# Strassen units of a fp32 transformer block: four of a unit's seven products in one PSUM bank, copied out by ScalarE

## The chip, the cores and the metric

The kernel runs on one core of a Trainium2 chip. The metric is the device time of one execution in microseconds (us). The times before are 2052.94, 2047.32 and 2055.45 us, with a median of 2052.94. The profile is of one execution on the chip. Engines are named as the profile names them: PE is TensorE's matmul, PEld its weight load, DVE is VectorE, ACT is ScalarE, POOL is GpSimd and SP is SyncE, which issues the DMAs.

## The reference

One decoder block over 1024 tokens of width 1024, all in fp32: a Mamba-2 (SSD) branch and a gated linear attention (GLA) branch merged by gates, cross attention to 256 memory tokens, and a SwiGLU FFN, with an RMSNorm ahead of each.

```
def hybrid_mixer(n, w_in, ...):
    proj = n @ w_in
    z, xBC, dt_raw, q, k, v, r, a1, g_ssd, g_gla = jnp.split(proj, idx, axis=-1)
    y_ssd = ssd_mixer(z, xBC, dt_raw, conv_w, conv_b, dt_bias, A_log, D_skip, ssd_norm)
    y_gla = gla_mixer(q, k, v, r, a1, gla_w_a2, gla_b_a, gla_norm)
    merged = jax.nn.sigmoid(g_ssd) * (y_ssd @ w_up_ssd) + jax.nn.sigmoid(g_gla) * (y_gla @ w_up_gla)
    return merged @ w_o

def swiglu(n, w_ffn_in, w_ffn_out):
    g, u = jnp.split(n @ w_ffn_in, 2, axis=-1)
    return (jax.nn.silu(g) * u) @ w_ffn_out

h = h + hybrid_mixer(rmsnorm(h, norm_mix), ...)
h = h + mem_cross_attention(rmsnorm(h, norm_xattn), rmsnorm(mem, norm_mem), w_xq, w_xkv, w_xo)
h = h + swiglu(rmsnorm(h, norm_ffn), w_ffn_in, w_ffn_out)
return rmsnorm(h, norm_final)
```

## The kernel before

**Precision.** An fp32 product is made of three matmuls in the faster fp32r format: both factors are split into a high and a low part, and `hi*hi`, `hi*lo` and `lo*hi` are summed in PSUM. For a weight, ScalarE copies out the high part `whi` (L217) and VectorE or POOL subtracts it from the weight to get `wlo` (most subtractions and additions of VectorE and POOL have line 73, that of a helper that counts their load). `whi` and `wlo` lie in rings of three buffers.

**Units.** The projections out of `w_in` and the FFN's gate and up projections are cut into 48 Units of 256 output columns by 1024 tokens (26 in `w_in`, 22 in the FFN). A Unit computes its 2 x 2 block product with the seven products of the Strassen-Winograd scheme instead of eight. Products are called B11, B21, B22 and T1 to T4 by their right-hand operand: Bij is a block of the input, T1 to T4 are sums and differences of such blocks, held ready, already split, as `B11h`, `B11l`, `T1h` and so on by the class Operands. The left-hand sums of weights (`sa`, or `raw` in place) are made by VectorE or POOL shortly before they are split. A product is twelve matmuls, four steps of the inner dimension times three; it is one [128, 512] tile in one PSUM bank. The four results of a Unit are the quarters q(i, j) of a buffer `o` (i is the half of the columns, j that of the tokens).

**Banks and evacuation.** There are four buffers `acc` for products (and four `bank` for all else). A Unit names three for itself, and two products that share a bank are added up in it, since only the first matmul of a bank clears it. So in bank x B21 is summed onto B11, in w B22 onto T1, and in y T3 onto T2 and T4 onto both. Behind each product the bank's sum so far is taken out: a copy by ScalarE behind B11 (L348) and B21 (L350), an addition into a quarter by VectorE behind the other five. PE may write a bank's next product only when the sum before has been taken out. A quarter that has had its last part is handed on: q(0, 0) behind B21, q(1, 1) behind T3, q(1, 0) behind T4, and q(0, 1) behind B22 or T2, whichever is later.

**Order.** `group` issues the products of one Unit in the order SPACED, or those of two Units together (the FFN's first gate and up) in the order CHAIN, product by product in turn. `singles` does Units one after the other. `run` mixes the Units' steps with a side job at a given rate: the preparation of decays and gates (`ssd_prep`, `gla_prep`) beside the four z Units, the convolution of the Unit before (`conv`) beside each of six xBC Units, the SSD scan of sixteen chunk-and-group steps beside nine Units, the GLA scan beside six. Splitting a weight and taking out a product are written with a raised priority (`ahead`). In the end a scheduler fixes the order of instructions on each engine ahead of time: each engine then works strictly through its own list, and an instruction that waits holds up those behind it.

**Lines the text speaks of.** L799, L800, L804 and L807 are the bias, abs, Exp and Ln of `gla_prep` (`gx`, `gy`), L463 the Silu of a z quarter, L728 that of a convolved channel row `cv`, L893 to L895 are the decay of an SSD step (eight Relu into `e`, Exp of `e`, Exp of `csb`, which a DMA brings). ScalarE needs another table in some changes of function, an ACT_TABLE_LOAD. L51 is every matmul, L55 every transpose.

Of the kernel before, what the change touches and what calls it, by code (L numbers as in the profile page):

```python
# [12 lines left out]
AF = mybir.ActivationFunctionType  # L13
# [24 lines left out]

CHAIN = ("B11", "B21", "T1", "B22", "T2", "T3", "T4")
SPACED = ("B11", "T1", "T2", "B21", "T3", "B22", "T4")  # L40


class Tensor:
# [35 lines left out]
def block_kernel(ctx: ExitStack, tc: tile.TileContext, t: dict, out: bass.AP):  # L79
    nc = tc.nc  # L80
    now = [0.0]
    PE, ACT, SP = Tensor(nc.tensor, now), nc.scalar, nc.sync
    DVE, POOL = Meter(nc.vector, now, 0.06, 1.04e-3), Meter(nc.gpsimd, now, 0.08, 2.25e-3)

    def either(ap, slack=0.0):

        return POOL if POOL.after(ap) - slack < DVE.after(ap) else DVE
# [34 lines left out]
    def acc():  # L122
        return ps.tile([P, 512], F32, name="acc", tag="acc", bufs=4)

    def bank(dt=F32):
        return ps.tile([P, 512], dt, name="bank", tag="bank", bufs=4)

    add = lambda e, o, a, b: e.tensor_tensor(o, a, b, ALU.add)
    sub = lambda e, o, a, b: e.tensor_tensor(o, a, b, ALU.subtract)
    mul = lambda e, o, a, b: e.tensor_tensor(o, a, b, ALU.mult)  # L130
    ahead = lambda: tc.high_priority(offset=AHEAD)
# [10 lines left out]
    def slot(key, shape=(P, 2, TOK), dt=F32, name="sl"):  # L142
        pl, n = slots[key]
        return pl.tile(list(shape), dt, name=name, tag="sl", bufs=n)
# [71 lines left out]
    def split(src, hi, lo, e=None):  # L216
        ACT.activation(hi, src, AF.Copy)  # L217
        sub(e or DVE, lo, src, hi)

    def wring():  # L220
        hi = wp.tile([P, 528], F32R, name="whi", tag="whi", bufs=3)
        lo = wp.tile([P, 528], F32R, name="wlo", tag="wlo", bufs=3)
        return hi, lo

    class Operands:
# [14 lines left out]
        def __init__(s, hb, kh, first=None, key="op", swap=0, last_key=None, order=None):  # L240
            s.B, s.kh, s.key, s.done, s.swap = {}, kh, key, 0, swap
            s.order = order or tuple(s.PLAN)
            s.last_key = last_key or key
            s.steps = s.build(hb, kh, first or (lambda *a: None))
# [7 lines left out]
        def __getitem__(s, name):  # L252
            s.upto((s.order.index(name) + 1) * s.kh)
            return s.B[name]

        def build(s, hb, kh, first):
            blk = hb if callable(hb) else lambda: hb
            for name in s.order:
                new, of, comb = s.PLAN[name]
                o = s.B[name] = [slot(s.last_key if name == "T4" else s.key, (P, kh, HALF), F32R, name=name + x) for x in "hl"]  # L260
                for k in range(kh):
# [8 lines left out]
    class Unit:  # L270
# [1 line left out]

        BANK = {"B11": "x", "B21": "x", "T1": "w", "B22": "w", "T2": "y", "T3": "y", "T4": "y"}

        def __init__(s, W, row0, c0, kh=4, post=None, key="aux", okey=None, side=None):
            s.W, s.row0, s.c0, s.kh, s.post, s.key, s.okey, s.side = W, row0, c0, kh, post, key, okey or key, side or key
# [30 lines left out]
        def q(s, i, j):  # L309
            return s.o[:, i, half(j)]  # L310
# [4 lines left out]

        def step(s, name, B, cs=ALL, again=False):
            s.load()
            kh = s.kh
            if name == "B11":
                s.banks, s.swap, s.u = {}, B.swap, False  # L320
                s.out()
            if again:
                wh, wl = s.w
            else:
                with ahead():
                    src = s.left(name)
                    hi, lo = wring()
                    s.w = wh, wl = [x[:, :kh * P].rearrange("p (k c) -> p k c", c=P) for x in (hi, lo)]
                    split(src, wh, wl)
            xh, xl = B[name]  # L330
            key = s.BANK[name]
            fresh = key not in s.banks
            if fresh:
                s.banks[key] = acc()
            p = s.banks[key]
            m = 0
            for k in range(kh):
                for x, y in ((wh, xh), (wh, xl), (wl, xh)):
                    PE.matmul(p[:, cs], x[:, k, :], y[:, k, cs], start=fresh and m == 0, stop=m == 3 * kh - 1,
                              skip_group_check=True)  # L340
                    m += 1
            s.evac(name, p, cs)

        def evac(s, name, p, cs):
            q = lambda i, j: s.q(i, j ^ s.swap)[:, cs]
            with ahead():
                if name == "B11":
                    ACT.activation(q(1, 0), p, AF.Copy)  # L348
                elif name == "B21":
                    ACT.activation(q(0, 0), p, AF.Copy)  # L350
                elif name == "T1":
                    add(DVE, q(1, 1), p, q(1, 0))
                elif name in ("B22", "T2"):
                    add(DVE, q(0, 1), p, q(0, 1) if s.u else q(1, 0))
                elif name == "T3":
                    add(DVE, q(1, 1), p, q(1, 1))
                else:
                    add(DVE, q(1, 0), p[:, cs], q(1, 0))
            s.done(name, cs)

        def done(s, name, cs=ALL):

            ij = {"B21": (0, 0), "T3": (1, 1), "T4": (1, 0)}.get(name)
            if name in ("B22", "T2"):
                ij = (0, 1) if s.u else None
                s.u = True
            if ij and cs == ALL:
                s.fin(ij[0], ij[1] ^ s.swap)

    class PartUnit(Unit):  # L370


        def __init__(s, base, *a, **kw):
            super().__init__(*a, **kw)
            s.base = base

        def evac(s, name, p, cs):
            q = lambda i, j: s.q(i, j ^ s.swap)
            b = lambda i, j: s.base.q(i, j ^ s.swap)
            get = lambda i, j: settle(s.base, i, j ^ s.swap)  # L380
            if name == "B21":
                get(0, 0)
                with ahead():
                    add(DVE, q(0, 0), p, b(0, 0))
                return s.done(name)
            super().evac(name, p, cs)
            for ij in {"T1": ((1, 1),), "B22": ((0, 1), (1, 0))}.get(name, ()):
                get(*ij)
                add(either(p), q(*ij), q(*ij), b(*ij))

    lag = [1]
    posts = {}
# [1 line left out]
    def settle(*key):  # L394

        k = key if key else next(iter(posts), None)
        if k in posts:
            del posts[k]
            u, i, j = k
            u.post(i, j, u.q(i, j))  # L400
# [9 lines left out]
    def group(units, B, then=(), nxt=None, frm=6, products=7):  # L410


        for u in units:
            u.load()
        then = list(then)
        many = len(units)
        for n, name in enumerate((CHAIN if many > 1 else SPACED)[:products]):
            for x, u in enumerate(units):
                u.step(name, B)
                if many > 1:  # L420
                    B.upto((n + 1) * B.kh - (-(x + 1) * B.kh // many))
                if n == 6 and nxt:
                    nxt.upto((x + 1) * nxt.kh // many)
                if n >= frm and then:
                    then.pop(0).load()
                while len(posts) > lag[0]:
                    settle()
                    if n < 4:
                        break
                yield  # L430
        for u in then:
            u.load()
# [106 lines left out]
    for k in range(NB):  # L539
        p = bank()  # L540
# [82 lines left out]
    B = Operands(hb, 4, xnorm)  # L623
# [85 lines left out]
    cs = cp.tile([P, P], F32, name="cs")  # L709
# [452 lines left out]
    def dense(no, ins, post, pre=lambda o, j: None, js=JS):  # L1162

        todo = [(o, j) for o in range(NB) for j in js]
        nxt = pre(*todo[0])
        for n, (o, j) in enumerate(todo):
            w = left[NB * no + o]
            cur, nxt = nxt, pre(*todo[n + 1]) if n + 1 < len(todo) else None
            p = acc()
            m = 0  # L1170
            for k in range(NB):
                for a, b in ((0, 0), (0, 1), (1, 0)):
                    PE.matmul(p, w[:, a, k], ins[k][:, b, half(j)], start=m == 0, stop=m == 3 * NB - 1)
                    m += 1
            with ahead():
                post(o, j, p, cur)
            yield
# [67 lines left out]
    def residual(store, stats, gain, put):  # L1245
        def post(o, j, p, q):
            add(DVE, q, p, q)
            SP.dma_start(store[o * P:(o + 1) * P, half(j)], q)
            put(o, j, q, col(gain, o))
            stats.take(j, q)  # L1250
        return post
# [98 lines left out]
    for n in range(len(at) + 2):  # L1350
        a = at[n] if n < len(at) else None
        b = at[n - 1] if 0 < n <= len(at) else None
# [55 lines left out]
    b_xo = blocks(o_xo)  # L1408
# [1 line left out]
    def put_xo(o, j, q, g):  # L1410
        ACT.activation(b_xo[o][:, half(j)], q, AF.Copy, scale=g)

    B = Operands(b_xo, 4, order=("B11", "T1", "B21", "B22", "T2", "T3", "T4"))
    for n, _ in enumerate(dense(4, i_xo, residual(h2_d, u_xo_stats, "norm_ffn", put_xo), gate_of(h1_d), js=(1, 0))):
        if n >= 8:
            B.upto(n - 7)
# [144 lines left out]
    for x, (n, k, kn) in enumerate(todo):  # L1561
        name = CHAIN[n]
# [4 lines left out]
        cs = slice(0, 256) if n == 6 else ALL  # L1567
# [9 lines left out]
    cs = slice(256, 512)  # L1577
# [43 lines left out]
```

## Time and profile before

| | us | share of the span |
|---|---|---|
| median of three runs | 2052.94 | |
| span of the profiled execution | 2047.0 | |
| PE busy | 1955.7 | 96% |
| VectorE busy | 1321.9 | 65% |
| ScalarE busy | 846.6 | 41% |
| POOL busy | 709.0 | 35% |

The span is the profiled execution's own time, from its first to its last instruction. A busy PE says that matmuls were under way, so the gaps on PE are the time in which something else set the pace; a row of a timeline gives the start, the duration, the engine, the line, the operation with its output and inputs, and in brackets the idle time ahead of it and what ended that. The stages, in order of time: memory keys and values and the input's norm (to 128), values (to 193), z Units (193 to 296), xBC Units with the convolution (296 to 424), SSD with Units (to 683), GLA with Units (to 869), dense products and attention (to 1377), the FFN's gate and up (to 1800), its down projection (to the end).

### The profile page before, as it was taken

The page shows a single profiled execution, that of the slowest core. Times are in us where ns is not written, and L with a number is a line of the kernel's source. Part 1 is how long each engine was busy: PE and PEld are TensorE (multiplying, and loading weights), DVE is VectorE, ACT ScalarE, POOL GpSimd, SP SyncE. Part 2 cuts the span into 40 slices and gives each one's busy share as a digit, 9 for nine tenths or more (in the row PEclk, how much of TensorE's full clock was granted, in tenths as well). Part 3 has the DMA queues.
Part 4 walks back from the last instruction along what each step waited for, and adds up shares of the span by engine and source line. Part 5 has one row for each costly group of instructions (what it writes and reads, how often), then busy time and mean ns, then how long its engine had stood idle before and what let it go on. Part 6 is the DMA issues. An engine that isn't in the chain of part 4 may idle for free.

```text
span 2047.0 us, 26356 instructions
## 1 busy us (share of the span) xinstructions
PE 1955.7 (96%) x9740; PEld 1624.7 (79%) x9740; DVE 1321.9 (65%) x1876; ACT 846.6 (41%) x1477; POOL 709.0 (35%) x513
## 2 busy tenths in 40 slices
PE   7589999999999999999999999999999999999998
PEld 7589777777777777878878888887888888887887
DVE  4975569878886665542454326568777777784465
ACT  6333753355553445442223225444333333354243
POOL 0733245445554221232224300154454454430002
PEclk9799999999999999999999999999999999999999
DMA  7532242345653665496675521332323422266463
GB/s 249 181 98 76 84 144 93 113 155 174 201 166 114 195 180 166 154 324 205 219 267 198 175 93 32 118 119 83 123 77 101 131 77 93 98 236 223 154 229 131
DMA packets 246436, 309.59 MB, mean 151 GB/s; under 512 B 18058, under 2 KB 165748, under 8 KB 246308
## 3 DMA queue, kind: packets, MB, share of 16 engines
q1 hardware_dynamic: 246308, 307.92, 45.6%
q8 instruction: 76, 1.25, 0.3%
q14 instruction: 52, 0.43, 0.1%
HBM read 211.07 MB, written 96.80 MB: 150 GB/s over the span
## 4 chain that ended last, share of the span: by engine, by line
PE 71%; DVE 9%; DMA 7%; issue 4%; ACT 4%; POOL 3%; SPq 1%; POOLq 0%; DVEq 0%; ACTq 0%
PE acc L51 62%; PE bank L51 8%; DVE wlo L73 2%; PE bank L55 1%; DVE cv L73 1%; DVE o L73 1%; DMA sr<-sr_d 1%; DMA csb<-cs_d 1%; DVE hs L73 1%; DMA bd<-bd_d 1%; SPq L644 1%; ACT e L893 1%; DMA ga<-ys_d 1%; POOL raw L73 1%; DMA fr<-act_d 1%
## 5 line engine op out<-in xcount | busy, mean ns | idle before, releaser
L51 PE MATMUL acc<-hl,wd 128*128 128x512 f32 x1920 | 443.8, 393 | 9.0 <-ACT hl L217 8.4
L51 PEld LDWEIGHTS acc<-hl,wd 128*128 128x128 f32 x1920 | 362.6, 189 | 86.0 <-ACT hl L217 9.7
L73 DVE TENSOR_TENSOR wlo<-raw,whi 128x512 fp32r<-128x512 f32 x272 | 236.6, 877 | 82.8 <-ACT whi L217 78.2
L217 ACT ACTIVATE whi<-raw 128x512 fp32r<-128x512 f32 x272 | 169.8, 628 | 255.1 <-PE acc L51 214.4
L73 DVE TENSOR_TENSOR o<-acc,o 128x512 f32<-128x512 f32 (+1 forms) x256 | 173.0, 677 | 120.1 <-PE acc L51 109.1
L73 POOL TENSOR_TENSOR sa<-raw 128x512 f32<-128x512 f32 x56 | 83.2, 1486 | 223.0 <-DMA raw<-in_w_ffn_out_dram 77.8
L51 PE MATMUL acc<-fs 128*128 128x512 f32 (+1 forms) x792 | 156.0, 356 | 1.9 <-ACT o L1516 1.7
L51 PEld LDWEIGHTS acc<-fs 128*128 128x128 f32 x792 | 130.7, 189 | 22.9 <-ACT o L1516 2.1
L73 POOL TENSOR_TENSOR sa<-sa,raw 128x512 f32<-128x512 f32 x48 | 73.3, 1527 | 160.0 <-DVE wlo L73 160.0
L217 ACT ACTIVATE fs<-fr 128x1024 fp32r<-128x1024 f32 (+1 forms) x84 | 80.1, 984 | 112.8 <-PE acc L51 42.2
L73 DVE TENSOR_TENSOR fs<-fr,fs 128x1024 fp32r<-128x1024 f32 (+1 forms) x84 | 99.0, 1206 | 39.8 <-ACT fs L217 39.5
L217 ACT ACTIVATE whi<-sa 128x512 fp32r<-128x512 f32 x96 | 60.4, 630 | 133.3 <-PE acc L51 67.7
L73 POOL TENSOR_TENSOR raw<-raw,sa 128x512 f32<-128x512 f32 x48 | 63.1, 1315 | 136.4 <-DVE wlo L73 136.4
L73 POOL TENSOR_TENSOR raw<-raw 128x512 f32<-128x512 f32 x68 | 101.8, 1502 | 9.5 <-DVE sa L73 6.2
L73 DVE TENSOR_TENSOR wd<-raw,wd 128x1024 fp32r<-128x1024 f32 x40 | 51.2, 1285 | 66.7 <-ACT wd L217 66.5
L73 DVE TENSOR_TENSOR wlo<-sa,whi 128x512 fp32r<-128x512 f32 x96 | 81.0, 844 | 11.0 <-ACT whi L217 9.8
L51 PE MATMUL acc<-T3h,whi 128*128 128x512 f32 x192 | 76.9, 401 | 10.7 <-DVE o L73 10.6
L73 DVE TENSOR_TENSOR ga<-acc,ga 128x512 f32<-128x512 f32 x64 | 43.6, 686 | 67.1 <-PE acc L51 47.1
L51 PE MATMUL acc<-B21h,whi 128*128 128x512 f32 x192 | 77.5, 404 | 3.7 <-ACT o L348 3.7
L51 PE MATMUL acc<-B22h,wlo 128*128 128x512 f32 x192 | 77.0, 401 | 1.9 <-DVE wlo L73 1.9
L51 PE MATMUL acc<-T4h,whi 128*128 128x512 f32 x192 | 76.7, 399 | 2.1 <-DVE o L73 2.1
L51 PE MATMUL acc<-T2h,wlo 128*128 128x512 f32 x192 | 76.4, 398 | 1.8 <-DVE wlo L73 1.8
(372 smaller groups left out, 4809.3 us busy)
## 6 DMA issues: line engine op xcount, KB each, us to landing
raw<-in_w_in_dram SPq DMA_DIRECT2D x26, 1024.0 KB, 5.7
raw<-in_w_ffn_in_dram SPq DMA_DIRECT2D x22, 1024.0 KB, 8.5
act_d<-o SPq DMA_DIRECT2D x77, 256.0 KB, 2.0
fr<-act_d SPq DMA_DIRECT2D x35, 512.0 KB, 6.2
raw<-in_w_ffn_out_dram SPq DMA_DIRECT2D x11, 1024.0 KB, 8.7
fr<-down_d SPq DMA_DIRECT2D x20, 512.0 KB
down_d<-raw SPq DMA_DIRECT2D x33, 256.0 KB, 2.9
raw<-in_w_xkv_dram SPq DMA_DIRECT2D x8, 1024.0 KB
```

The source lines that it names most:

```text
L51: return s.e.matmul(o, x, y, **kw)
L55: return s.e.transpose(o, x, i)
L73: return f(*a, **kw)
L217: ACT.activation(hi, src, AF.Copy)
L644: SP.dma_start(r_[:, :, o:o + n], w_in[512 * h:512 * h + 512, c0:c0 + n].rearrange("(k p) c -> p k c", p=P))
L893: ACT.activation(s.e[:, h], s.csb[:, h], AF.Relu, bias=cs[:, s.i0 + h:s.i0 + h + 1], scale=-1.0)
```

## The change

All seven products keep their operands and their matmuls. Banks and evacuations are dealt anew: B11, T2, T3 and T4 share the bank c and are summed up in it, T1 and B22 share w as before, and B21 has the bank x alone. ScalarE copies the bank's sum out behind B11 into q(0, 0), T1 into q(1, 1), T2 into q(0, 1) and T4 into q(1, 0); VectorE adds behind B21 into q(0, 0), T3 into q(1, 1) and B22 into q(0, 1). Per Unit these are four copies and three additions instead of two copies and five additions. A pair of Units now takes the order PAIRED; the operands ahead of the FFN are prepared in the same order. A class that nothing uses, PartUnit, is removed.

```
 SPACED = ("B11", "T1", "T2", "B21", "T3", "B22", "T4")
+PAIRED = ("B11", "T1", "B21", "T2", "T3", "B22", "T4")
...
-        BANK = {"B11": "x", "B21": "x", "T1": "w", "B22": "w", "T2": "y", "T3": "y", "T4": "y"}
+        BANK = {"B11": "c", "T2": "c", "T3": "c", "T4": "c", "T1": "w", "B22": "w", "B21": "x"}
...
                 if name == "B11":
-                    ACT.activation(q(1, 0), p, AF.Copy)
+                    ACT.activation(q(0, 0), p, AF.Copy)
                 elif name == "B21":
-                    ACT.activation(q(0, 0), p, AF.Copy)
+                    add(DVE, q(0, 0), p, q(0, 0))
                 elif name == "T1":
-                    add(DVE, q(1, 1), p, q(1, 0))
-                elif name in ("B22", "T2"):
-                    add(DVE, q(0, 1), p, q(0, 1) if s.u else q(1, 0))
+                    ACT.activation(q(1, 1), p, AF.Copy)
+                elif name == "T2":
+                    ACT.activation(q(0, 1), p, AF.Copy)
                 elif name == "T3":
                     add(DVE, q(1, 1), p, q(1, 1))
+                elif name == "B22":
+                    add(DVE, q(0, 1), p, q(0, 1))
                 else:
-                    add(DVE, q(1, 0), p[:, cs], q(1, 0))
+                    ACT.activation(q(1, 0), p, AF.Copy)
...
-        for n, name in enumerate((CHAIN if many > 1 else SPACED)[:products]):
+        for n, name in enumerate((PAIRED if many > 1 else SPACED)[:products]):
...
-    B = Operands(b_xo, 4, order=("B11", "T1", "B21", "B22", "T2", "T3", "T4"))
+    B = Operands(b_xo, 4, order=PAIRED)
```

The instructions that a whole program issues change little: on VectorE `o<-acc,o` goes from 248 to 152, on ScalarE `o<-acc` from 100 to 196, ScalarE's table loads go from 28 to 31, and ten `o<-o` move from VectorE (75 to 65) to POOL (29 to 39). But the scheduler's lists also change. Three places follow; line numbers behind the change are one more than before for L51, L55 and L217, and L728, L799, L800, L804, L807 and L463 have become L707, L778, L779, L783, L786 and L442.

ScalarE's list over one xBC Unit, before (`sa` and `raw` are weights to be split, L348 and L350 the copies behind B11 and B21):

```order
L217 ACTIVATE whi<-raw 128x512
L217 ACTIVATE whi<-sa 128x512 x2
L217 ACTIVATE whi<-raw 128x512
L348 ACTIVATE o<-acc 128x512
L728 ACTIVATE cv<-cv 128x1024
L217 ACTIVATE whi<-raw 128x512 x3
L350 ACTIVATE o<-acc 128x512
L728 ACTIVATE cv<-cv 128x1024
```

and of the change, where L361, L349, L353 and L355 are the copies behind T4 of the Unit before, B11, T1 and T2:

```order
L218 ACTIVATE whi<-raw 128x512 x2
L218 ACTIVATE whi<-sa 128x512
L361 ACTIVATE o<-acc 128x512
L218 ACTIVATE whi<-sa 128x512
L218 ACTIVATE whi<-raw 128x512
L349 ACTIVATE o<-acc 128x512
L707 ACTIVATE cv<-cv 128x1024
L218 ACTIVATE whi<-raw 128x512
L353 ACTIVATE o<-acc 128x512
L218 ACTIVATE whi<-raw 128x512
L355 ACTIVATE o<-acc 128x512
L707 ACTIVATE cv<-cv 128x1024
```

Each copy stands behind the split of the next weight, and T2's is ahead of the second Silu.

ScalarE's list in the z Units, around the first Exp of the gates, before:

```order
L217 ACTIVATE whi<-sa 128x512
L463 ACTIVATE o<-o 128x512
L804 ACT_TABLE_LOAD
L804 ACTIVATE gy<-gy 128x2048
L217 ACTIVATE whi<-raw 128x512
L348 ACTIVATE o<-acc 128x512
L807 ACT_TABLE_LOAD
L807 ACTIVATE gy<-gy 128x2048
L217 ACTIVATE whi<-raw 128x512
L799 ACTIVATE gx<-bank,cols 128x512 x3
```

and of the change, from right behind the Exp to the copy behind B11 of the third z Unit (L349; L361 is the copy behind T4 of the second):

```order
L218 ACTIVATE whi<-sa 128x512
L778 ACTIVATE gx<-bank,cols 128x512 x3
L442 ACT_TABLE_LOAD
L442 ACTIVATE o<-o 128x512
L786 ACT_TABLE_LOAD
L786 ACTIVATE gy<-gy 128x2048
L779 ACTIVATE gy<-gx 128x1024
L361 ACTIVATE o<-acc 128x512
L779 ACTIVATE gy<-gx 128x1024
L218 ACTIVATE whi<-sa 128x512
L218 ACTIVATE whi<-raw 128x512
L349 ACTIVATE o<-acc 128x512
```

Between Exp and the copy behind B11 there stood one split; now three `gx`, two table loads, a Silu, the Ln, two abs, a copy and three splits stand there. A little further on, both loads, the second Exp and the second Ln stand ahead of the split of T3's weight and of the copy behind T2.

PE's list where the SSD stage begins (`bank<-e,xd` is the first matmul of scan step 0, and `e` its decay), before, from the end of B21's matmuls:

```order
L51 MATMUL acc<-B21l,whi 128x512
L51 MATMUL acc<-B21h,wlo 128x512
L51 MATMUL acc<-B21h,whi 128x512
L51 MATMUL bank<-e,xd 64x128 x2
L51 MATMUL bank<-xc,bt 128x512
L51 MATMUL bank<-bc 128x128
```

and of the change, from the end of T1's:

```order
L52 MATMUL acc<-T1h,whi 128x512
L52 MATMUL acc<-T1l,whi 128x512
L52 MATMUL acc<-T1h,wlo 128x512
L52 MATMUL bank<-e,xd 64x128 x2
L52 MATMUL bank<-xc,bt 128x512
L52 MATMUL bank<-bc 128x128
```

Before, all twelve matmuls of T2 and ten of B21 stood ahead of the scan step; now they come behind it.

More of the change, by code (lines that the diff above doesn't have):

```diff
@@ L319, in step @@
             if name == "B11":
-                s.banks, s.swap, s.u = {}, B.swap, False
+                s.banks, s.swap = {}, B.swap
                 s.out()
@@ L347, in evac @@
                 if name == "B11":
-                    ACT.activation(q(1, 0), p, AF.Copy)
+                    ACT.activation(q(0, 0), p, AF.Copy)
                 elif name == "B21":
-                    ACT.activation(q(0, 0), p, AF.Copy)
+                    add(DVE, q(0, 0), p, q(0, 0))
                 elif name == "T1":
-                    add(DVE, q(1, 1), p, q(1, 0))
-                elif name in ("B22", "T2"):
-                    add(DVE, q(0, 1), p, q(0, 1) if s.u else q(1, 0))
+                    ACT.activation(q(1, 1), p, AF.Copy)
+                elif name == "T2":
+                    ACT.activation(q(0, 1), p, AF.Copy)
                 elif name == "T3":
                     add(DVE, q(1, 1), p, q(1, 1))
+                elif name == "B22":
+                    add(DVE, q(0, 1), p, q(0, 1))
                 else:
-                    add(DVE, q(1, 0), p[:, cs], q(1, 0))
+                    ACT.activation(q(1, 0), p, AF.Copy)
             s.done(name, cs)
         def done(s, name, cs=ALL):
[L363 to L366, printed above, removed]
+            ij = {"B21": (0, 0), "T3": (1, 1), "B22": (0, 1), "T4": (1, 0)}.get(name)
             if ij and cs == ALL:
                 s.fin(ij[0], ij[1] ^ s.swap)
[L370 to L389, printed above, removed]
     lag = [1]
```

## The prediction

> **What bounds the kernel now.** I read the page's busy shares first, then a stretch of the span without gaps, then whom PE waits for.
>
> ```profile
> span 2047.0 us, 26356 instructions
> PE 1955.7 (96%) x9740; PEld 1624.7 (79%) x9740; DVE 1321.9 (65%) x1876; ACT 846.6 (41%) x1477; POOL 709.0 (35%) x513
> ```
>
> PE is busy for 96% and the change leaves its matmuls as they are, so all that can be won are PE's 91 us of gaps, and only those behind an evacuation of a product. The span is 2047.0 us; the runs of this kernel are 2047.32, 2052.94 and 2055.45, so the profiled execution lies 5.9 under their median. I work out a change against the profiled execution and add it to the median. The FFN shows a stretch without any gap:
>
> ```profile
> 1415.50:1800.00 384.50, 384.50 (x1663) 312.76 (x1662) 294.19 (x360) 130.90 (x221) 179.82 (x119) 1.00 0.29 97
> L73 DVE TENSOR_TENSOR o<-acc,o 128x512 f32<-128x512 f32 x248 | 169.8, 686 | 109.5 <-PE acc L51 98.5 <-issue 10.4 <-ACT o L348 0.7
> L348 ACT ACTIVATE o<-acc 128x512 f32<-128x512 f32 x48 | 27.9, 580 | 1.7 <-PE acc L51 1.7
> ```
>
> The columns behind a stretch are its length, then busy time of PE, PEld, DVE, ACT and POOL, then PE's clock. 384.50 us hold 1663 matmuls, so one takes 0.231 us and a product of twelve 2.77 us. An add behind a product takes VectorE 0.69 us, a copy takes ScalarE 0.58 us. Where PE waits for the adds is seen in the conv stage and the stage ahead of it:
>
> ```profile
> PE acc L51 <- DVE o L73: 10.6, 8, 1.5
> PE acc L51 <- DVE wlo L73: 3.7, 2, 1.9
> PE acc L51 <- ACT whi L217: 0.3, 1, 0.3
> 316.40:337.60 21.20, 19.69 (x85) 15.73 (x85) 18.76 (x19) 7.41 (x11) 10.55 (x7) 1.00 0.29 99
> ```
>
> These are 193 to 443 us: 10.6 of the 14.6 us are waits for `o`, and a conv unit keeps VectorE busy for 88% of its 21.20 us, ScalarE for 35%.
>
> **B: six conv units.** One unit on VectorE, and PE beside it:
>
> ```profile
> 328.76 3.33 DVE L73 SCALAR_TENSOR_TENSOR cv<-o,cols,cv 128x1023 f32<-128x1023 f32 x2
> 332.01 0.68 DVE L73 TENSOR_TENSOR wlo<-raw,whi 128x512 fp32r<-128x512 f32 x1
> 332.62 0.68 DVE L73 TENSOR_TENSOR o<-acc,o 128x512 f32<-128x512 f32 x1
> 333.22 2.00 DVE L73 SCALAR_TENSOR_TENSOR cv<-o,cols,cv 128x1022 f32<-128x1022 f32 x1
> 335.14 1.77 DVE L73 TENSOR_TENSOR wlo<-raw,whi 128x512 fp32r<-128x512 f32 x1
> 336.83 0.68 DVE L73 TENSOR_TENSOR o<-acc,o 128x512 f32<-128x512 f32 x1
> ...
> 332.42 0.39 PE L51 MATMUL acc<-T2h,wlo 128*128 128x512 f32 x1
> ...
> 335.66 0.39 PE L51 MATMUL acc<-B22l,whi 128*128 128x512 f32 x1
> 337.56 0.50 PE L51 MATMUL acc<-T3h,whi 128*128 128x512 f32 x1 [1.51 <-DVE o L73]
> ```
>
> T2 leaves PE at 332.8, but its add starts at 336.83, behind T1's add, a conv step and a wlo; T3 wants T2's bank at 335.89 and gets it at 337.56. That is 1.67 us, and the idle rows of the six units read 1.48 to 1.53. Now ScalarE empties the bank. Ahead of T2's copy in its row stand a Silu, two whi, and T1's copy:
>
> ```profile
> 330.93 1.06 ACT L728 ACTIVATE cv<-cv 128x1024 f32<-128x1024 f32 x1 [2.75 <-DVE cv L73]
> 334.17 0.63 ACT L217 ACTIVATE whi<-raw 128x512 fp32r<-128x512 f32 x1 [1.66 <-POOL raw L73]
> ```
>
> The Silu ends at 332.0. Even if both whi, T1's copy and T2's copy all come behind T2's end at 332.8, that is 332.8 + 2 x 0.53 (pitch of whi) + 0.5 + 0.58 = 334.9, 1.0 before T3 wants the bank. The next thing late is VectorE: it loses two adds per unit (1.2 us of pitch) and has 17.6 us of work in a unit that now takes 19.5. Carrying the rows along the new order, B21's wlo is the tightest, 0.6 us ahead of PE. So **6 x 1.67 = -10.0 us**. Bounds: -11 (also the starts behind the stalls) and 0 (a wlo that comes 0.6 + 1.67 later takes the stall's place); -10 is nearer, as ScalarE and wlo both have slack in these rows.
>
> **A: the z units beside the gate preparation.** ScalarE runs Exp and Ln of 2048 columns there.
>
> ```profile
> 231.87 1.20 PE L51 MATMUL bank<-a1T,wa 48*128 48x512 f32 x4
> 241.56 0.96 PE L51 MATMUL bank<-a1T,wa 48*128 48x512 f32 x3
> ...
> 238.30 1.28 ACT L804 ACT_TABLE_LOAD   x1
> 239.59 1.91 ACT L804 ACTIVATE gy<-gy 128x2048 f32<-128x2048 f32 x1
> 246.16 1.83 ACT L799 ACTIVATE gx<-bank,cols 128x512 f32<-128x512 f32 x3
> 248.39 2.00 ACT L800 ACTIVATE gy<-gx 128x1024 f32<-128x1024 f32 x2
> ...
> 255.27 0.50 PE L51 MATMUL acc<-B22h,wlo 128*128 128x512 f32 x1 [1.91 <-DVE wlo L73]
> 256.77:260.18 3.41, 3.41 (x10) 2.65 (x9) 3.12 (x5) 3.38 (x3) 1.56 (x3) 0.50 0.88 352
> ```
>
> A stretch of 3.41 us at half clock follows the 1.91 us gap (ten matmuls instead of 15): it costs 1.7 us. Before, the stage loses 5.5 us of idle (14.6 less the six conv stalls of about 1.51), some 1.0 in the starts of those five, and 1.7: 8.2. In the new order PE makes the first four gate products two products earlier, at 231.87 - 2 x 2.77 = 226.3, and the next three (before: at 241.56, behind T1) ahead of the unit's last product, so all the gate work reaches ScalarE sooner. From there ScalarE's new row runs gx and abs to 231.0, whi to 231.6, load and Exp to 235.2 (1.28 + 1.83), whi and three gx to 237.5, load and Silu to 239.4, load and Ln to 242.5, abs, T4's copy, abs to 245.0, then whi of T2 and of B21, and only then B11's copy, to 246.6. T2 needs that copy. PE leaves T1 at about 241.2, a little before the 241.56 of now, as those three products are done: a wait of 5.4, and 1.7 for the half clock behind. Behind it, T3's whi and T2's copy stand behind Exp and Ln with both loads (6.2 us): they end at 256.8 where PE arrives at about 254.2, so 2.6, and 1.7 again. 11.4 - 8.2 = **+3.2 us**; bounds 0 (Exp slips behind the copies as waits fall out) and +6 (a third gap like those). All that is queued behind the late copies are whi, and PE waits for these too, so nothing hides it.
>
> The Trainium skill, "TensorE: Matmul & The Clock Gate", Part 1, has the clock fall after an idle window of about 3.4 us. The trace disagrees, with a half clock right behind a gap of 1.91 us; by the page the second gap would cost no clock, A would come to +1.5 and the sum to 1.7 us less than mine.
>
> **C: entry of the SSD stage.** Before, T2 and ten matmuls of B21 stand on PE ahead of scan 0; now it stands right behind T1.
>
> ```profile
> 433.81 2.45 ACT L893 ACTIVATE e<-csb,cs 128x128 f32<-128x128 f32 x8 [2.25 <-DMA csb<-cs_d]
> 437.28 1.28 ACT L894 ACT_TABLE_LOAD   x1
> 438.57 1.06 ACT L894 ACTIVATE e<-e 128x1024 f32<-128x1024 f32 x1
> 439.54 1.05 ACT L895 ACTIVATE csb<-csb 128x1024 f32<-128x1024 f32 x1
> 439.67 1.36 DVE L73 TENSOR_TENSOR e<-e,cbm 128x1024 f32<-128x1024 f32 x1 [1.56 <-ACT e L894]
> ...
> 436.77 0.40 PE L51 MATMUL acc<-T2h,whi 128*128 128x512 f32 x1
> ...
> 441.99 0.44 PE L51 MATMUL bank<-e,xd 128*64 128x128 f32 x4
> ```
>
> PE is through T1 at 436.77, scan 0 has `e` at 441.0 (439.67 + 1.36): 4.2 us, and 1.7 for the clock: **+5.9 us**. T2 and B21 then follow without a wait, so nothing comes back. Bounds 0 (csb lands earlier by as much, since it is issued behind the conv stage's last stores) and +6 (a second gap between the scan's own matmuls is no part of it).
>
> **D: SSD stage, 443 to 683.** Sixteen decays, each 2.45 + 1.28 + 1.06 + 1.05 = 5.8 us on ScalarE, now run among four copies per unit instead of two. A bank's copy has 2.77 us of another product as its cover: a copy behind a whole decay is 3.1 late. In the new rows I find one such place at 2.5 (part of a decay) and one at 1.4; against them stand 2.1 us of waits for `o` that PE has there now and that mostly go. **+2**, bounds -3 (all present small gaps go) and +15 (rival below).
>
> ```profile
> PE acc L51 <- DVE o L73: 2.1, 2, 1.1
> ```
>
> **E: GLA, 683 to 869, 0** (-3 to +3): its copies' covers stay, and PE waits there for other things. **F: start of the FFN.** The pair's second product is now T1 and not B21.
>
> ```profile
> 1387.03 0.79 PE L51 MATMUL acc<-B21h,whi 128*128 128x512 f32 x1 [3.66 <-ACT o L348]
> 1386.58:1390.00 3.42, 2.98 (x7) 2.40 (x8) 3.42 (x6) 1.92 (x4) 0.00 (x0) 0.50 0.84 266
> ```
>
> T1's operands are there earlier, so these 3.7 and 1.7 go; but the sums' product with `ones` and T1's wlo now come behind VectorE's operand splits, a wait of about 2.6. **-2.5**, bounds -5.4 and 0. Ten operand combinations move from VectorE to POOL:
>
> ```profile
> L73 POOL TENSOR_TENSOR o<-o 128x512 f32<-128x512 f32 x29 | 48.8, 1687 | 26.2 <-DVE o L73 12.4 <-DVE B21l L73 5.0 <-ACT o L1411 4.5
> ```
>
> At 1.7 us each they lie under the FFN's matmuls, which run without a gap, and cost nothing; two of them in front of the pair's first products would eat up F, which is in its upper bound.
>
> **Everything else, 0**: in the FFN PE has no gap, and T2's copy there has 2.77 us of B21 against 0.58. Three more table loads, 3.8 us, are in A or under ScalarE's 59% of idle time.
>
> Sum: 3.2 - 10.0 + 5.9 + 2 + 0 - 2.5 = **-1.4**, so a span of 2045.6 and, on the median, **2051.5 us**.
>
> **Rivals.** *Full gain*: A, C and D cost nothing, because copies lead in ScalarE's row wherever PE waits. For it speaks ScalarE's 41%, against it the row orders at A and C. -10.0 - 2.5: 2040.4 us. *The stall comes back elsewhere in a conv unit*: VectorE is at 17.6 of 19.5 us, and a wlo that comes 2.3 us late puts PE where the add had it. B is 0: 2061.5 us. The 0.6 us of slack at B21 speak for it, the two adds less against. *Slower, ScalarE's queue*: with three banks for seven products, one of which serves four, PE waits for every copy that stands behind a decay in the SSD stage, 3.1 us each. It is slower by over 0.5% (10.3 us, about what a measurement of this kernel can tell from no change) from five such places in sixteen on: five are +15.5 in place of D's +2, 2065.0 us, and four, 2061.9, are not enough. For it speaks that a decay takes 5.8 of ScalarE, against it that ScalarE is busy in only 32.16 of 57 us there:
>
> ```profile
> 443.00:500.00 57.00, 55.83 (x360) 42.92 (x359) 49.44 (x89) 32.16 (x70) 29.92 (x24) 1.00 0.53 165
> ```
>
> The Trainium skill, "Perfetto Trace Analysis", Matmuls, asks that independent products rotate through different banks so that the evacuation of one lies beside the next; this is the rule that speaks against the change, and the conv stalls, at a bank that T2 and T3 share, agree with it. That the change doesn't do what it says is excluded: the rows show 96 adds fewer and 96 copies more.
>
> **How the numbers follow.** Forecast 0.46 (2044 to 2058), full gain 0.20, stall back in conv 0.16, ScalarE's queue 0.18. Below 2038 lies full gain's lower third with F at -5.4, 0.07; above 2066 half of the queue's chance, 0.09; so the range is 2038 to 2066. Faster by over 0.5% (under 2042.7) are two thirds of full gain and 0.05 of the forecast's tail: 0.18. Slower (over 2063.2) are 0.12 of the queue and 0.04 of the stall: 0.16. The rest, 0.66, is within.
>
> **What would show it.** B: no gap before T3 in six units, their period 19.5 to 19.6 us instead of 21.2. A: T2 waiting about 5 us for a copy near 241 with a half clock behind. C: PE idle for about 4 us ahead of the first `bank<-e,xd`. D: waits for ScalarE's copies of over 4 us in sum. F: the 3.66 us gap gone. I am wrong if the conv period stays near 21, if A and C show no wait for ScalarE, or if D's waits pass 10 us.

## The result, and the profile after

The changed kernel takes 2039.45 us in the median (2037.77 to 2042.53, 7 runs) against 2049.43 us (2046.38 to 2055.45, 7 runs) for the kernel before. The ratio is 0.9949, with a 95% interval from 0.9934 to 0.9965. The profiled execution has a span of 2037.7 us and took 2039.45 us, so some 1.75 us lie around a span. The 2047.0 us of before were thus an execution of about 2049, which is the median of seven runs; the median of three, on which the prediction stands, was 3.5 us above that.

All the prediction's stages can be read from where the same matmul starts in both traces; of a product T4 it is the tenth of its twelve (in the pair, of the second T4):

| start of | before | after | shift |
|---|---|---|---|
| T4 of the first z Unit | 213.94 | 216.67 | +2.73 |
| T4 of the first xBC Unit (Unit 5) | 302.89 | 310.35 | +7.46 |
| T4 of Unit 11, behind the convolutions | 430.22 | 430.17 | -0.05 |
| 200th matmul of the dense products | 923.57 | 918.38 | -5.19 |
| 840th matmul of the dense products | 1076.24 | 1063.64 | -12.60 |
| last matmul of the dense products | 1377.41 | 1364.79 | -12.62 |
| T4 of the FFN's first pair | 1426.17 | 1418.86 | -7.30 |
| T4 of Unit 47 | 1795.39 | 1787.83 | -7.57 |
| 198th matmul of the FFN's down projection | 1861.82 | 1852.52 | -9.30 |

The first 2.73 us are not the change's: the first z Unit starts 3.40 us later already (196.47 us, before 193.07), and the stages ahead of it have the same instructions. Then z loses 4.7, the conv Units win 7.5, SSD, GLA and the entry of the dense products together win 5.1, the dense products win 7.4 at one place, the pair loses 5.3, and the end wins 1.7 by a wait of that size at 1846.92 us that one execution had and the other had not.

The page of the changed kernel, its groups of evacuations, and a conv Unit as a stretch (columns as in the prediction):

```profile
span 2037.7 us, 26292 instructions
PE 1958.7 (96%) x9740; PEld 1626.2 (80%) x9740; DVE 1265.7 (62%) x1773; ACT 897.1 (44%) x1576; POOL 726.2 (36%) x520
L74 DVE TENSOR_TENSOR o<-acc,o 128x512 f32<-128x512 f32 x152 | 104.1, 687 | 77.8 <-PE acc L52 77.6
L355 ACT ACTIVATE o<-acc 128x512 f32<-128x512 f32 x48 | 27.9, 581 | 0.0
316.40:336.38 19.98, 19.73 (x86) 15.64 (x85) 17.95 (x17) 8.23 (x13) 11.31 (x6) 1.00 0.29 105
```

96 additions of 0.69 us left VectorE and 96 copies of 0.58 came to ScalarE, as forecast; the Unit is 19.98 us long, not 21.20. In it a small wait is left, on the timelines of PE, ScalarE and POOL:

```profile
322.12 0.50 PE L52 MATMUL acc<-B22h,whi 128*128 128x512 f32 x1 [0.25 <-ACT whi L218]
321.44 0.63 ACT L218 ACTIVATE whi<-raw 128x512 fp32r<-128x512 f32 x1 [2.68 <-POOL raw L74]
321.98 0.58 ACT L355 ACTIVATE o<-acc 128x512 f32<-128x512 f32 x1
318.61 2.80 POOL L74 TENSOR_TENSOR raw<-raw,sa 128x512 f32<-128x512 f32 x1 [4.81 <-DVE wlo L74]
```

T2's copy (L355) is no longer waited for. B22's weight is: POOL makes it, starts at 318.61 behind a wlo and needs 2.80 us. This takes 0.4 us per Unit (0.64 from start to start in place of 0.23), so 6 x (1.67 - 0.42) = 7.5.

In the z Units there are two long waits, as forecast, but only the first has the forecast cause (ScalarE, VectorE, PE, and the stretch at half clock):

```profile
244.07 1.91 ACT L786 ACTIVATE gy<-gy 128x2048 f32<-128x2048 f32 x1
245.89 1.04 ACT L779 ACTIVATE gy<-gx 128x1024 f32<-128x1024 f32 x1
246.84 0.58 ACT L361 ACTIVATE o<-acc 128x512 f32<-128x512 f32 x1
...
248.78 0.62 ACT L218 ACTIVATE whi<-raw 128x512 fp32r<-128x512 f32 x1
249.30 0.58 ACT L349 ACTIVATE o<-acc 128x512 f32<-128x512 f32 x1
...
248.30 5.50 DVE L74 TENSOR_TENSOR_SCAN gy<-keep,gx 128x1024 f32<-128x1024 f32 x2
253.72 0.66 DVE L74 TENSOR_TENSOR wlo<-sa,whi 128x512 fp32r<-128x512 f32 x1
...
249.45 0.79 PE L52 MATMUL acc<-B21h,whi 128*128 128x512 f32 x1 [4.11 <-ACT whi L218]
254.44 0.79 PE L52 MATMUL acc<-T2h,wlo 128*128 128x512 f32 x1 [2.92 <-DVE wlo L74]
...
247.91:258.15 10.24, 5.79 (x13) 4.10 (x14) 10.24 (x7) 10.15 (x12) 8.75 (x6) 0.50 0.10 38
```

PE waits 4.1 us for B21's split, which stands on ScalarE behind the Ln; B11's copy (L349, done at 249.88), for which the forecast had T2 wait, lies right behind it. The second wait, 2.9 us for T2's wlo, is VectorE's: that subtraction stands behind two scans of the gate preparation, 5.50 us. 10.24 us run at half clock.

What the prediction did not have stands in the dense products. These are whom PE waits for there before (866 to 1075 us), the wait itself, and what ScalarE waits for ahead of it; the last row is the same split after the change, where PE waits for nothing in these products:

```profile
PE acc L51 <- ACT hl L217: 8.4, 2, 4.2
PE acc L51 <- DVE hl L73: 0.5, 1, 0.5
...
884.59 5.77 PE L51 MATMUL acc<-hl,wd 128*128 128x512 f32 x17 [4.20 <-ACT hl L217]
883.91 1.97 ACT L217 ACTIVATE hl<-ga 128x512 fp32r<-128x512 f32 x3 [10.36 <-DMA ga<-ys_d]
...
1067.31 0.79 PE L51 MATMUL acc<-hl,wd 128*128 128x512 f32 x1 [4.24 <-ACT hl L217]
1065.68 1.06 ACT L217 ACTIVATE wd<-raw 128x1024 fp32r<-128x1024 f32 x1 [8.41 <-DMA down_d<-raw]
1066.64 0.61 ACT L217 ACTIVATE hl<-ga 128x512 fp32r<-128x512 f32 x1
```

```profile
1054.87 1.06 ACT L218 ACTIVATE wd<-raw 128x1024 fp32r<-128x1024 f32 x1 [6.25 <-DMA down_d<-raw]
```

Both times the split `hl` of an input is late on ScalarE. At 884 it waits for a fetch of `ys_d`. At 1067 it stands behind `wd`, the split of a dense weight, and that waits for a buffer from which a side job has yet to store (`down_d<-raw`: block sums of the FFN's last weight, made ahead of time, in four buffers shared with the dense weights). Why both went is the question of the experiments.

### The profile page after: what moved, and what is told of

Read it like the earlier page. It is cut to its first block, busy times and chain, and to the rows that moved or that the text cites. A ratio compares the mean times of both kernels' runs of the same rounds, so it can differ in the third digit from the quotient of the medians.

```text
span 2037.7 us, 26292 instructions
## 1 busy us (share of the span) xinstructions
PE 1958.7 (96%) x9740; PEld 1626.2 (80%) x9740; DVE 1265.7 (62%) x1773; ACT 897.1 (44%) x1576; POOL 726.2 (36%) x520
## 4 chain that ended last, share of the span: by engine, by line
PE 63%; DVE 3%; DMA 3%; ACT 2%; POOL 1%; issue 1%; SPq 0%; POOLq 0%; ACTq 0%; DVEq 0%
PE acc L52 56%; PE bank L52 6%; PE bank L56 1%; DMA sr<-sr_d 1%; DMA yg_d<-sr 1%; DVE wlo L74 0%; DMA bd<-bd_d 0%; DMA raw<-in_w_in_dram 0%; POOL ssum L74 0%; DMA fr<-act_d 0%; DVE o L74 0%; ACT o L1027 0%; DVE S L74 0%; DVE T3l L74 0%; ACT L982 0%
## 5 line engine op out<-in xcount | busy, mean ns | idle before, releaser
L74 DVE TENSOR_TENSOR wlo<-raw,whi 128x512 fp32r<-128x512 f32 x272 | 250.7, 925 | 119.9 <-ACT whi L218 119.7
L74 DVE TENSOR_TENSOR o<-acc,o 128x512 f32<-128x512 f32 (+1 forms) x160 | 107.3, 674 | 88.4 <-PE acc L52 88.2
L74 POOL TENSOR_TENSOR raw<-raw,sa 128x512 f32<-128x512 f32 x48 | 75.6, 1575 | 86.5 <-DVE wlo L74 86.4
L74 POOL TENSOR_TENSOR o<-o 128x512 f32<-128x512 f32 x39 | 63.8, 1638 | 59.6 <-DVE o L74 35.1
L52 PE MATMUL acc<-B22h,whi 128*128 128x512 f32 x192 | 77.2, 402 | 2.4 <-ACT whi L218 2.4
```

What stands on the lines that cost most here:

```text
L52: return s.e.matmul(o, x, y, **kw)
L74: return f(*a, **kw)
```

## The experiments

All twelve runs are one kernel: the changed one, in which each Unit can also have the banks, copies and adds of before; two of them slow a side job down as well. With all Units and the pair's order set to the form of before (the run with the slower side job), PE's 9740 matmuls come in the order of before, and the other engines' lists are the same up to the second dense product, in which the job is slowed down.

```
+        OLD_BANK = {"B11": "x", "B21": "x", "T1": "w", "B22": "w", "T2": "y", "T3": "y", "T4": "y"}
...
-            key = s.BANK[name]
+            key = (s.OLD_BANK if s.old else s.BANK)[name]
...
+                if s.old:
+                    if name == "B11":
+                        ACT.activation(q(1, 0), p, AF.Copy)
+                    elif name == "B21":
...
+    for u_ in ...:
+        u_.old = True
```

The table gives the ratio to the kernel before on the same chip, and the shifts against the trace of before, worked out as in the table above: from T4 of the first z Unit to that of Unit 5 (z), to that of Unit 11 (conv), to the 200th dense matmul (scans and entry), from the 780th to the 960th (dense wait), and from the last to the pair's T4 (pair).

| run | ratio (95%) | z | conv | scans, entry | dense wait | pair |
|---|---|---|---|---|---|---|
| the change | 0.9949 (0.9934 to 0.9965) | +4.7 | -7.5 | -5.1 | -7.4 | +5.3 |
| conv alone | 0.9973 (0.9955 to 0.9992) | +1.5 | -5.6 | +3.3 | +0.4 | -0.2 |
| last gate Unit alone | 0.9993 (0.9979 to 1.0007) | 0.0 | 0.0 | -3.2 | +1.3 | -0.2 |
| FFN pair alone | 1.0024 (1.0010 to 1.0039) | 0.0 | 0.0 | -1.1 | -6.4 | +5.7 |
| GLA Units alone | 0.9991 (0.9977 to 1.0004) | +1.5 | +0.1 | +0.4 | -4.0 | -0.1 |
| SSD Units alone | 0.9978 (0.9960 to 0.9995) | 0.0 | -0.8 | -3.2 | -7.6 | 0.0 |
| all but the SSD Units | 1.0017 (0.9999 to 1.0036) | +4.6 | -5.8 | +0.8 | -5.8 | +5.5 |
| all but the pair | 0.9928 (0.9907 to 0.9950) | +4.7 | -7.3 | -6.1 | -5.7 | +0.4 |
| all but z and the pair | 0.9921 (0.9891 to 0.9950) | +1.5 | -7.3 | -5.7 | -5.9 | -0.1 |
| pair's order alone | 1.0001 (0.9983 to 1.0019) | +1.5 | 0.0 | -0.1 | -0.8 | +0.2 |
| before, side job slower | 0.9982 (0.9967 to 0.9997) | +1.5 | 0.0 | 0.0 | -7.6 | -0.1 |
| all but z and pair, side job slower | 0.9905 (0.9873 to 0.9937) | 0.0 | -7.4 | -6.3 | -7.6 | -0.3 |
| all but z and the pair, again | 0.9899 (0.9876 to 0.9923) | 0.0 | -7.5 | -5.6 | -7.6 | -0.3 |

The +1.5 in z stands in kernels whose z Units are those of before, so it belongs to no edit.

**Conv alone.**

```
+    for u_ in zu + ru + qk + gs[:1] + gs[1:] + gg[:3] + gg[3:]:
+        u_.old = True
```

> Only the six xBC Units take the new banks and copies, all others stay as before. Local theory (each stage's change is its own): the six T3 waits of 1.5 us go and leave a wait of 0.25 us ahead of B22, so the stage is 6 x 1.25 = 7.5 us shorter and the kernel 7.5 us faster; the two waits for ScalarE's hl in the dense stage (8.4 us) stay. Rival (the dense stage's gain is a knock-on of anything that shifts the stages ahead of it): those two waits go here too, some 20 us faster in all.

The ratio 0.9973 is 5.5 us, and both dense waits stayed (4.2 and 3.6 us): the local theory. In its profile the stage is 5.6 us shorter, but +1.5 in z and +3.3 behind the stage take nearly all of it back: the span is 2046.6 us against 2047.0. So the time agrees in the median of ten runs (2036.2 to 2049.3) and not in the profiled one, and what costs the 3.3 us is open. The stage's size is 5.6 and not 7.5 since a convolution runs beside the Unit that follows: the sixth lies beside the first r Unit, which is old here and has a T3 wait of 1.91 us at 418.67. The run of all but the SSD Units has the same.

**The last gate Unit alone.** The same list without `gg[3:]`, and with `xu`.

> Only the last gate Unit, the one beside which the first dense product's input is fetched, takes the new banks and copies. If the two hl waits of the dense stage (884.59 and 1067.31 us before) went because this Unit's copies let the fetches through, the kernel is about 13 us faster. Rival: they went because the GLA scan ended earlier against the Units (its last store issued at 846.33 us, not 861.42); then both stay here and the time is within 2 us of before.

Both waits stayed (2.8 and 3.7 us), and the ratio's interval holds 1. This Unit's copies are not what let the fetches through.

**The pair alone.** All Units of the projections and the later FFN Units old.

> Only the first FFN pair takes the new banks, the new order and the operands in the new order. Local theory: the start of the FFN loses 5.8 us as in the changed kernel (waits for the sums, for whi and wlo of T1 and T2, and 6.8 us at half clock in place of 3.4), so 5 to 6 us slower than before. Rival, the prediction's own: 2.5 us faster, and what the changed kernel lost there came from the stages ahead.

+5.7 us in its stage and 1.0024 in time, so the local theory. The dense wait at 1067 was gone in this profile (-6.4), though nothing ahead of it was changed: it comes and goes from one execution to another.

**The GLA Units alone.**

```
+    for u_ in zu + xu + ru + qk + gs[:1] + gg[3:]:
+        u_.old = True
```

> Only the six Units beside the GLA scan take the new banks and copies. If the earlier end of the GLA scan against the Units lets the first dense input be fetched earlier, both hl waits of the dense stage go: 10 to 14 us faster, with the scan's last store well ahead of the last gate Unit's start. Rival (the last gate Unit's own copies, or the SSD stage): the waits stay and the time is within 3 us of before.

The expectation failed: the waits were smaller but there (1.5 us at the first place, 2.1 at the second), and the ratio's interval holds 1. In PE's list the GLA scan still ends behind Unit 25.

**The SSD Units alone, and all but the SSD Units.**

```
+    for u_ in zu + xu + gs[1:] + gg[:3] + gg[3:]:
+        u_.old = True
```

```
+    for u_ in ru + qk + gs[:1]:
+        u_.old = True
```

> Only the nine Units beside the SSD scan take the new banks and copies. In PE's list the GLA scan then ends behind Unit 24 as in the changed kernel, and not behind Unit 25. If that earlier end is what frees the first dense product's input, the hl waits at 884.59 and 1067.31 us of before go with their half clock, and the kernel is 10 to 13 us faster. Rival (the dense stage's waits come and go with the DMAs' times, whatever the list): the kernel is within 3 us of before, with one of the waits in its profile.

> The changed kernel with the nine Units beside the SSD scan left as before; the GLA scan ends behind Unit 25 again. If the SSD stage carries the gain through that, the rest sums up to z +4.7, conv -7.5, FFN pair +5.5: 0 to 5 us slower than before. Rival (the parts add up by stage and the SSD Units are worth little): 8 to 10 us faster than before, as the changed kernel.

With the SSD Units alone PE waits for no `hl` in the dense products. Without them it waits for 5.4 us, and nothing is left of the gain: 1.0017. The rows of whom PE waits for from 866 to 1075 us in the latter:

```profile
PE acc L52 <- ACT hl L218: 5.4, 4, 2.7
PE acc L52 <- DVE hl L74: 0.8, 1, 0.8
```

SyncE's queue shows where the changed kernel differs. Before, the last store of the GLA scan (`yg_d<-sr`) is issued at 861.42, and the fetches of the first dense input come behind it and between the stores of the last gate Unit; after the change it is 846.33:

```profile
861.42 0.37 SPq L1062 DMA_DIRECT2D yg_d<-sr  x1
865.02 2.71 SPq L1112 DMA_DIRECT2D ga<-ys_d  x6
...
870.82 4.92 SPq L464 DMA_DIRECT2D gg_d<-o  x1
875.83 1.58 SPq L1112 DMA_DIRECT2D ga<-ys_d  x3
877.50 0.40 SPq L464 DMA_DIRECT2D gg_d<-o  x1
878.00 5.00 SPq L1112 DMA_DIRECT2D ga<-ys_d  x3
```

```profile
846.33 0.37 SPq L1041 DMA_DIRECT2D yg_d<-sr  x1
...
850.47 1.47 SPq L1091 DMA_DIRECT2D ga<-ys_d  x3
...
860.37 2.84 SPq L1091 DMA_DIRECT2D ga<-ys_d  x4
```

Earlier fetches alone do not explain why PE has no wait. The input that the 37th dense matmul needs (the row of ScalarE) comes 14.6 us behind the first dense matmul before the change, and 15.9 us behind it after:

```profile
869.29 0.62 PE L51 MATMUL acc<-hl,wd 128*128 128x512 f32 x2
872.51 7.88 PE L51 MATMUL acc<-hl,wd 128*128 128x512 f32 x34
```

```profile
864.56 4.59 PE L52 MATMUL acc<-hl,wd 128*128 128x512 f32 x18
874.54 4.27 PE L52 MATMUL acc<-hl,wd 128*128 128x512 f32 x18
881.42 2.89 PE L52 MATMUL acc<-hl,wd 128*128 128x512 f32 x12
880.45 1.96 ACT L218 ACTIVATE hl<-ga 128x512 fp32r<-128x512 f32 x3 [6.68 <-DMA ga<-ys_d]
```

What lies in between has changed. Before, twelve matmuls of the last gate Unit (T4) stand between the first and the 37th dense matmul; after, 36 do (B22, T3 and T4). These 24 more, 5.5 us at 0.231, are work that PE has while the input is under way, and more than the wait of 4.2. The first six inputs are fetched some 15 us earlier, and in PE's list the dense product begins ahead of these three products.

In the six kernels whose SSD Units are changed (the change, SSD alone, the two without the pair or without z and the pair, and the last two runs) the GLA scan ends behind Unit 24 in PE's list, 22 matmuls of the last Unit (SSD alone) or 36 stand in that place, and none of their profiles has the wait at 884. In the eight others it ends behind Unit 25, twelve or none stand there, and seven have that wait as one of 2.7 us or more; in the eighth, GLA alone, it is spread over several of up to 1.5. The size on the clock is only part of the expectation for SSD alone: 0.9978 is 4.5 us, and its ten runs fall into five from 2037.0 to 2044.0 and five from 2046.9 to 2048.0, of which the profile shows the first kind.

**All but the pair; all but z and the pair.** Old are `gu[0]` and its order, and then `zu` too.

```
-        for n, name in enumerate((PAIRED if many > 1 else SPACED)[:products]):
+        for n, name in enumerate((CHAIN if many > 1 else SPACED)[:products]):
...
-    B = Operands(b_xo, 4, order=PAIRED)
+    B = Operands(b_xo, 4, order=("B11", "T1", "B21", "B22", "T2", "T3", "T4"))
```

> The changed kernel with the first FFN pair, its order and its operands' order left as before. If the pair costs 5.3 us at the start of the FFN, this is 5 to 6 us faster than the changed kernel, so 13 to 15 us faster than before. Rival (the pair's loss comes from what stands ahead of it): as the changed kernel, 8 to 10 us faster than before.

> As the run without the pair, and the four z Units left as before too. If ScalarE's Exp and Ln ahead of the copies cost 4.7 us in the z Units, this is a further 4 to 5 us faster, 17 to 20 us faster than before. Rival (the gaps there only change places): no faster than the run without the pair.

> The version with old z Units and old FFN pair once more, beside the other three. Theory: 0.989 to 0.993 of the time before, with a spread of runs under 4 us since neither dense wait is left. Rival: the first look was a lucky one, and it is no better than the changed kernel's 0.995.

0.9928, and 0.9921 and 0.9899 in two runs of the second: 2035.80, 2033.78 and 2027.38 us, where the kernel before took 2049.97, 2049.97 and 2045.45. The pair's cost is shown by its stage (+0.4 in place of +5.3) and by the pair alone; by time it is not told apart, as the intervals of this run and of the change overlap (up to 0.9950, from 0.9934). What z costs is not told apart from the pair's run by time (0.9928 against 0.9921, intervals over each other), but by its stage, where 4.7 us become 0.0 or 1.5. The spread of the second run is 8.1 us, twice what was expected. This version beats both kernels: in its second run the interval (0.9876 to 0.9923) lies below that of the change.

**The pair's order alone.** All banks old, PAIRED and its operands' order kept.

> The kernel before with only the order of the first FFN pair changed (B11, T1, B21, T2, T3, B22, T4) and its operands prepared in that order; all banks, copies and adds as before. If the order costs the 5.5 us at the start of the FFN (T1's split and the sums stand behind the splits of the operands), the profile loses 4 to 6 us between the last dense matmul and the pair's end. Rival (the copies on ScalarE among the operands' splits cost it): within 2 us of before there.

+0.2 us: the order alone costs nothing, against the expectation's first theory. Whom PE waits for from 1364 us to the pair's end, in the changed kernel and with the order alone (`ssum` and `diag` belong to a norm whose small matmuls stand among the pair's):

```profile
PE acc L52 <- ACT whi L218: 2.6, 5, 1.0
PE bank L52 <- DVE ssum L74: 2.2, 1, 2.2
PE acc L52 <- DVE wlo L74: 1.4, 3, 0.9
```

```profile
PE bank L52 <- DVE diag L74: 2.2, 1, 2.2
PE acc L52 <- ACT whi L218: 1.3, 2, 1.0
PE bank L52 <- DVE ssum L74: 0.8, 1, 0.8
```

So the loss comes with the new banks and their copies, and PE's timeline of the changed kernel shows how:

```profile
1383.73 0.80 PE L52 MATMUL acc<-T2h,whi 128*128 128x512 f32 x1 [0.29 <-ACT whi L218]
...
1406.16 0.40 PE L52 MATMUL acc<-B21h,whi 128*128 128x512 f32 x1
```

The pair does not run in the order written. B11 and T1 of two Units fill the four `acc` buffers, of which the two of bank c are now held until T4; B21, with a bank of its own, finds room only when a B22 has freed w. So T1 and T2 come right behind B11 (T2 at 1383.7, B21 at 1406.2; before B21 at 1387.0, T1 at 1391.7, T2 at 1406.5), while VectorE and ScalarE still split the operands. The new banks with the old order were not tried: there B22 stands ahead of T2, and the addition behind B22 needs what T2's copy has laid down. That the order forced by the banks makes the loss, and not ScalarE's additional copies among the operands' splits, is read from the timeline; no run parts the two.

**The side job, slower.** Before, and the best version, with

```
-    run(dense(1, i_yg, post_yg, pre_yg), (early, 1.0))
+    run(dense(1, i_yg, post_yg, pre_yg), (early, 0.5))
```

> The kernel before with the side job that sums the blocks of the FFN's last weight mixed into the second dense product at half the rate; it shares four buffers with the dense weights. If the hl wait at 1067.31 us comes from a dense weight's split that waits for this job's store, the wait and its half clock go (7.4 us in the profile of before) and the time falls by 3 to 7 us, with runs less spread. Rival (the wait is the load's of the next weight): the wait stays, same time.

> The version without the z Units' and the pair's change, with the side job of the run before at half the rate in the second dense product. In that version the hl wait at 1067 us is gone already, so the theory gives the same time within 2 us. Rival (the job holds up more than that wait): 3 us or more faster than the version without it.

In the kernel before the wait at 1067 went with its half clock (-7.6 us in the profile), the other `hl` wait stayed, and the time is 0.9982 of before:

```profile
PE acc L52 <- ACT hl L218: 4.1, 1, 4.1
```

The ten runs spread over 7.6 us, the 23 of before over 13.6. One profile without the wait would not be enough, as the pair alone had none either; but the row of ScalarE names the store, and the time follows. So the cause is shown: the dense weight's split waits for the side job's store, in a buffer they share. The version without z and the pair gains nothing by the slower job (0.9905 against 0.9899), since it no longer has that wait.

## Why the prediction was right in its range and wrong in its reasons

The time lies in the range and the sign is right, near the rival called full gain (2040.4); that rival's reasons are not what happened, as A and C did cost time. That the time is in the range, 1.45 us above its lower end, is luck: the stages that the prediction foresaw came to 4.7 - 7.5 + 1.0 + 5.3 = +3.5 us in the profile, not to -1.4, and the gain comes from two waits, 13.5 us, that stand in none of its terms. The median it started from was also 3.5 us high.

- **B**, -10.0, was right in mechanism and mis-sized: -7.5 over the six waits. T2's copy has the slack that was worked out, and the next thing late is not B21's wlo but B22's weight on POOL, 0.4 us per Unit.
- **A**, +3.2, came out at +4.7: 4.1 and 2.9 us of waits in place of 5.4 and 2.6, and three stretches at half clock in place of two. The first is the mechanism forecast, ScalarE's queue of Exp, Ln and loads, but at 249.45 us and for B21's split, not near 241 for the copy. The second was forecast on ScalarE too and came from VectorE's scans; that its size fits is chance. The working also has a slip: 231.6 + 1.28 + 1.83 is 234.7, not 235.2.
- **C**, +5.9, is mis-sized: PE reaches scan 0 at 436.7 as before, but waits 2.1 us for `e` and not 4.2, since csb came earlier (ScalarE starts on `e` at 431.84 us, before at 433.81). A stretch at half clock follows as forecast, so about +3.8.

```profile
437.69 1.23 DVE L74 TENSOR_TENSOR e<-e,cbm 128x1024 f32<-128x1024 f32 x1 [1.55 <-ACT e L873]
438.97 0.66 PE L52 MATMUL bank<-e,xd 128*64 128x128 f32 x4 [2.10 <-DVE e L74]
```

- **C, D and E** together were +7.9. Measured are -5.1 with the entry's wait in it; that wait was 4.4 us from start to start and a stretch of half clock worth 1.7, so without it they are +1.0. With C at +3.8, D and E together are about -2.8 in place of +2. D's sign, over 4 us of waits for copies, did not come: from 435 to 683 us PE waits for none. In GLA two copies behind T2 are waited for, 2.8 us, where E had none; the stage's waits in sum are 6.4 us, before 6.5.
- **F**, -2.5, was +5.3: the step that failed is "so these 3.7 and 1.7 go". They went, and the waits for T1's and T2's whi and wlo and for the sums took their place, 6.2 us, with 6.83 us at half clock in place of 3.41. I had priced one wait, of 2.6, and no clock, though A charges 1.7 for a gap of that size (and 3.7 + 1.7 - 2.6 is 2.8, not 2.5), because I took the pair to run in its written order; four buffers let it run only with T2 ahead of B21.
- **Everything else, 0**, is the step that mattered: -7.4 at the dense products' second wait, and -6.1 at their first. I left both out because no evacuation stands behind them ("only those behind an evacuation of a product"); but the SSD Units' change lets the GLA scan end a Unit earlier in the list, the first dense input is fetched earlier, and more of the last Unit's matmuls stand beside the rest of that fetch. It is shown that this wait goes with the SSD Units and stays without them. That it goes by way of the scan's end is read from the lists and from SyncE's queue; no edit moved that end alone, nor the last Unit's matmuls alone, so it is argued. The second wait's cause is shown by the side job. After the change the split still waits 6.25 us for a store, but that store is issued 5.1 us ahead of PE's matmul (1052.49, 1057.56); before, it is issued 0.5 us ahead of PE's gap (1062.59, 1063.07). Why that wait is less frequent with the changed SSD Units (a wait of over 2 us in none of their six profiles, and in five of the seven others that have the side job at its old rate) is open, as it also came and went between executions.
- The parts don't add up: SSD alone (-4.5 us by its ratio) and all but SSD (+3.5) give -1, the whole change -10.5 by its ratio. In the profiles, counted from T4 of the first z Unit, they are nearer: -9.7 and -1.2 against -12.0. What joins them is open.

## What to carry to other kernels

A stage that the edit doesn't touch is not worth nothing: ask what the edit does to the order of side jobs ahead of it, which fetch waits for their end, and what work lies beside that fetch; list every wait of the kernel's busiest engine first, also those that seem to be no concern of the change. Copies moved to an engine that works in order are free where only short work stands there (the conv Units), and cost where a table load and a long function stand ahead (z Units). A bank that serves more products is held longer, and where two such groups share the buffers (the FFN pair) they run in another order than the written one: change a shared routine stage by stage and keep the old form where it was better.

## What the runs showed of the hardware

The half clock came after gaps well under its own length of 3.41 us, and where a gap lies decides as much as its size. In each trace the stretches at half clock start, from 190 us on, whole multiples of 3.41 us apart (before: at 256.77, 710.75, 799.49, 884.83, 1065.73 and 1386.58 us), so they follow a fixed grid. I cut PE's time into stretches of that grid and added up its idle time in each, small gaps too. From 190 to 2030 us, every stretch at full clock with 1.73 us of idle or more is followed by one at half clock, and none with 1.71 or less is: about half of a stretch is the limit here (the ends of matmuls are modelled, so its last digits are not sure). This sorts the gaps that their size does not. The 1.91 us ahead of 255.27 lie in one stretch, and half clock follows. The 1.57 ahead of 708.77 make 1.73 with the small gaps beside them, and it follows. The 1.81 ahead of 270.52 leave 1.71 in one stretch, the 1.88 ahead of 753.20 are cut by a border at 751.71 and leave 1.52, and the conv Units' gaps are 1.5: none follows. The Trainium skill, "TensorE: Matmul & The Clock Gate", Part 1, has it after an idle window of about 3.4 us that runs freely; the fixed grid agrees, but the whole of it need not be idle.
